# Query, key and value products of two attention heads made among the delta rule's fillers and kept in DRAM

## The chip, the cores and the metric

The kernel runs on one core of a Trainium2 chip. A core has TensorE (matmuls into PSUM), VectorE, ScalarE and GpSimd (element-wise work), and SyncE, which issues nearly all DMAs here from one queue in order. The five run on their own and wait for each other by semaphores. The metric is the device time of one execution in microseconds (us); the kernel before takes 2994.62 us, the median of 3 runs (2992.21 to 2998.93).

## The reference, cut to what matters

One layer of an encoder block in float32, 1024 tokens of width 1024. A normed input is projected once; the columns of the projection feed differential attention (8 heads), a bidirectional gated delta rule (8 heads), and gates. The two branches are projected, gated, summed and projected again; 16 experts with expert choice follow.

```python
h = rmsnorm(x, norm1_w[l])
p = jnp.einsum('bsd,dn->bsn', h, w_in[l])
(qa, ka, va, qkv_g, z, a_f, a_b, b_f, b_b, gate_a, gate_g) = jnp.split(p, split_at, axis=-1)
qa = apply_rope(qa.reshape(b, s, DA_HEADS, 2, DA_DH), cos, sin)
ka = apply_rope(ka.reshape(b, s, DA_HEADS, 2, DA_DH), cos, sin)
...
oa = diff_attention(qa, ka, va, lam)          # softmax(q1 k1) - lam softmax(q2 k2), times v
...
o_fwd = gated_delta_rule_chunked(qg, kg, vg, g_f, beta_f)
o_bwd = flip(gated_delta_rule_chunked(flip(qg), flip(kg), flip(vg), flip(g_b), flip(beta_b)))
...
merged = jax.nn.sigmoid(gate_a) * ya + jax.nn.sigmoid(gate_g) * yg
x = x + jnp.einsum('bsd,de->bse', merged, w_out[l])
x = x + expert_choice_ffn(h2, w_router[l], w_gate[l], w_up[l], w_down[l])
out = rmsnorm(x, norm_f_w)
```

## The kernel before, in words

**How the program is recorded.** Every part of the work is a Python generator (a task). The class `Emit` holds a clock for each engine and a table of costs; of all operations whose inputs are known it records the one that could start first by these clocks, and at a tie the one of the smaller priority number. What comes out is one fixed order of instructions for each engine. On the chip each engine works through its order and waits where an operand is not there. All matmuls of the program come from line 403 (`mm`), all transposes on TensorE from line 407 (`tr`), ScalarE's work from line 415, VectorE's products and sums from line 421, GpSimd's from 425, VectorE's three-operand operations from 446, its reductions from 463, and SyncE's DMAs from 495. So a row of the profile is told by its operands.

**Tags.** A tag is a named place in SBUF with a number of slots; `e.new(tag)` waits until a slot is free and nothing that lies over it is live. `xp` (two slots, the inputs of the delta rule's convolution) and `ax` (two slots of 1024 columns, the attention's projected query, key or value, transposed) lie over each other in block B3. `QS`, `K1`, `K2` (rotated queries and keys) lie in block B1 and can only be taken once all the delta rule's buffers there are done.

**Dense jobs.** A projection job (`proj_ns`) makes a 128 x 1024 slice of the projection: two halves of 512 columns, each 8 x 3 matmuls of 128x512 in float32r (the input and the weights are split in a high and a low part, tiles A0 and A1, and three of the four products are taken), so 48 matmuls a job, named psum<-A,W. `Dense` keeps two queues. `main` holds the delta rule's q, k, v, z jobs and then the attention's jobs, three for each head; `fill` holds the 16 gate jobs, each of which ends in a tanh by ScalarE and a store of 256 KB for each half to `dgate`. The loader looks at the first two of `main`, and takes the first of `fill` when neither may start. The worker has the lowest priority (9), so that dense matmuls go where the planner sees TensorE free.

**The seam.** The attention's jobs may start when the last delta head has its q, k and v (`gdn_close`) and, from head 2 on, when 4 rows of the heads before are done. A job's product goes to an `ax` slot; then `rope` (for q and k) copies it by four DMAs into `rot` with the halves of 32 swapped, multiplies by cosine and sine and adds (three products of 128x1024 on VectorE), and splits the result in high and low parts (ScalarE casts, VectorE and, for a key's second copy, GpSimd subtract); `vrows` transposes the values on TensorE. A head's rows start when it has q, k and v. Three lanes take the 64 rows (8 heads x 8 blocks of 128 queries) in order: scores (8 matmuls psum<-B 128x512), two maxima on VectorE, two exponentials on ScalarE, a scaling, a difference, 8 transposes, 8 matmuls with the values. So a row is 24 instructions of TensorE in the planner's count. Meanwhile `finish` of delta head 7 norms its output (products on VectorE), transposes it by two times four transposes on TensorE, gates it and stores it to `dog`.

Of the kernel before, what the change touches and what calls it, by code (L numbers as in the profile page):

```python
# [8 lines left out]
F32 = mybir.dt.float32  # L9
# [9 lines left out]
S, D, H, P = 1024, 1024, 8, 128  # L19
# [5 lines left out]
AHEAD = 2  # L25
TAIL = 4
LANES = 3
PACE = (4, 4, 4)


# [30 lines left out]
class Buf:  # L61
    def __init__(self, v, slot):
        self.v, self.slot = v, slot
# [654 lines left out]
def proj_ns(g, evac, wait=None):  # L718

    e = g.e  # L720

    def job(hi, lo):
        hh, hl = g.hh, g.hl
        for sh in range(2):
            if not g.hready[sh]:
                yield lambda: g.hready[sh]
            ps = yield from e.new("mm", [P, 512])
            if sh == 0:
                dst = (yield from wait()) if wait else None
            sl = slice(sh * 512, sh * 512 + 512)  # L730
            for d in range(8):
                e.mm3(ps.v, hi[:, d, :], lo[:, d, :], hh[:, d, sl], hl[:, d, sl], d == 0, d == 7)
                yield
            e.urgent(True)
            yield from evac(sh, ps, dst)
            e.free(ps)
            e.urgent(False)
            yield
    return job
# [149 lines left out]
class Head:  # L889
# [8 lines left out]
    def has(self, *f):  # L898
        return all(x in self.flags for x in f)

    def set(self, f):
        self.g.e.then(lambda: self.flags.add(f))
# [347 lines left out]
class Attn:  # L1250
    def __init__(self, g, h, prev):
        self.g, self.h = g, h
        self.pp = prev.prev if prev else None
        self.prev = prev
        self.flags = set()
        self.rows_left = NT

    def has(self, *f):
        return all(x in self.flags for x in f)
# [8 lines left out]
    def jobs(self):  # L1268
        g, h, e = self.g, self.h, self.g.e
        out = []  # L1270
        for j in (0, 1, 2):
            def ok(j=j):
                return g.gdn_close and (not self.pp or 16 - self.pp.rows_left - self.prev.rows_left >= PACE[j])
            def evac(sh, ps, x, j=j):
                e.cp(x[:, sh * 512:sh * 512 + 512], ps.v)
                if sh == 1:
                    e.spawn(self.vrows(x) if j == 2 else self.rope(j, x), 2)
                yield
            out.append((g.ins["w_att"][h, j], ok, proj_ns(g, evac, lambda: e.new("ax", [P, S])), "ax"))
        return out  # L1280

    def vrows(self, x):
        g, e = self.g, self.g.e
        self.v = yield from e.new("v", [P, NT, P])
        self.last("v", "ax")
        for half in range(2):
            pt = yield from e.new("ga", [P, 512])
            for i in range(4):
                t = half * 4 + i
                e.tr(pt[:, i * P:(i + 1) * P], x[:, t * P:(t + 1) * P], g.ident.v)  # L1290
            e.cp(self.v[:, half * 4:half * 4 + 4, :], pt.v.rearrange("p (t x) -> p t x", x=P))
            e.free(pt)
            yield
        e.free(x)
        self.set("v")
# [131 lines left out]
def attn_lane(g, rows, i):  # L1427
    e = g.e
    while rows:
        at, qt = rows.popleft()  # L1430
        yield lambda: at.has("q", "k", "v")
        if qt == 0:
            yield from at.start()
        yield lambda: at.has("start")
        yield from at.row(qt)
    e.then(lambda: setattr(g, "lanes", g.lanes + 1))
    if i == 0:
        yield lambda: g.attn_done == g.heads
        e.close("ga", "sc", "p", "pT", "rsm", "o", "o2", "osm", "aq", "cos", "sin")
        e.free(g.cos, g.sin)  # L1440
# [86 lines left out]
def w_out(g):  # L1527
    e = g.e
    yield lambda: g.lanes == LANES
    for n in range(8):  # L1530
# [566 lines left out]
def body(tc, ins, out, dbg=None, heads=H):  # L2097
    nc = tc.nc
    g = Ctx()
    g.nc, g.tc, g.ins, g.out, g.dbg, g.heads = nc, tc, ins, out, dbg or {}, heads  # L2100
    with ExitStack() as ctx:
# [3 lines left out]
        dp = ctx.enter_context(tc.tile_pool(name="dr", bufs=1, space=DRAM))  # L2105
        e = g.e = Emit(nc, pool, psum)
# [3 lines left out]
        g.dw = [dp.tile([16, 64, 2, 16], F32, name=f"dw{i}") for i in range(2)]  # L2110
        g.dog = dp.tile([2, H, P, S], F32, name="dog")
        g.doa = dp.tile([2, H, P, S], F32, name="doa")
        g.dgate = dp.tile([2, 8, P, S], F32, name="dgate")
        g.dyg = dp.tile([2, 8, P, 512], F32, name="dyg")
        g.dx2 = dp.tile([S, D], F32, name="dx2")
# [28 lines left out]
        d = g.dense = Dense(g)  # L2144
        d.main.append(logit_job(g))
        prev, hs = None, []
        for h in range(heads):
            prev = Head(g, h, prev)
            hs.append(prev)
            j = prev.jobs()  # L2150
# [10 lines left out]
        for h in range(heads):  # L2161
            prev = Attn(g, h, prev)
            ats.append(prev)
            j = prev.jobs()
            d.main.extend(j)

        g.hT_jobs = 0
        d.main = deque(using_hT(g, j) for j in d.main)
# [12 lines left out]
        rows = deque((at, qt) for at in ats for qt in range(NT))  # L2181
        for i in range(LANES):
            e.spawn(attn_lane(g, rows, i), 1)
# [8 lines left out]
        x = Experts(g)  # L2192
# [79 lines left out]
```

## Time and profile before

| what | us |
|---|---|
| median of 3 runs | 2994.62 |
| the runs | 2992.21 to 2998.93 |
| the profiled execution, whole | 3000.25 |
| its span, first to last instruction | 2998.0 |
| delta rule with its projections, to | about 959 |
| attention and the branches' projections, to | about 1800 |
| work before the experts, to | about 1930 |
| experts, to the end | about 2998 |

The span is what the profile's times count from; 2.25 us of the profiled execution lie around it. The limits of the stages are read from the table of stretches and the timelines. Busy shares are of the span. A matmul's record lasts longer than its turn, since matmuls are pipelined: what counts is from one start to the next. The number in brackets behind a timeline row is how long the engine stood still before it, and who ended that.

### The profile page before, as it was taken

The page shows a single profiled execution, that of the slowest core. Times are in us where ns is not written, and L with a number is a line of the kernel's source. Part 1 is how long each engine was busy: PE and PEld are TensorE (multiplying, and loading weights), DVE is VectorE, ACT ScalarE, POOL GpSimd, SP SyncE. Part 2 cuts the span into 40 slices and gives each one's busy share as a digit, 9 for nine tenths or more (in the row PEclk, how much of TensorE's full clock was granted, in tenths as well). Part 3 has the DMA queues.
Part 4 walks back from the last instruction along what each step waited for, and adds up shares of the span by engine and source line. Part 5 has one row for each costly group of instructions (what it writes and reads, how often), then busy time and mean ns, then how long its engine had stood idle before and what let it go on. Part 6 is the DMA issues. An engine that isn't in the chain of part 4 may idle for free.

```text
span 2998.0 us, 40541 instructions
## 1 busy us (share of the span) xinstructions
PE 2855.3 (95%) x14712; PEld 2384.8 (80%) x14712; DVE 2351.6 (78%) x3954; ACT 1760.6 (59%) x2683; POOL 555.9 (19%) x443
## 2 busy tenths in 40 slices
PE   7999999999999899999999998999999999999996
PEld 6787887787788778888888787688888888888885
DVE  7768778677765877877763439899999999999998
ACT  4435445445434566776672322577777777777775
POOL 3322222122222211211125422100000000000001
PEclk9999999999999999999999998999999999999998
DMA  4223322322322111111267833999999999999996
GB/s 141 51 63 92 85 53 65 88 60 62 83 57 79 51 50 51 49 50 43 67 193 238 267 131 137 419 411 386 384 378 388 388 388 388 385 386 381 380 375 244
DMA packets 203642, 598.73 MB, mean 200 GB/s; under 512 B 84386, under 2 KB 102306, under 8 KB 154290
## 3 DMA queue, kind: packets, MB, share of 16 engines
q1 hardware_dynamic: 189858, 562.06, 51.5%
q0 software_dynamic: 13584, 34.08, 4.2%
q8 instruction: 115, 1.88, 0.3%
q14 instruction: 85, 0.70, 0.1%
HBM read 535.19 MB, written 52.49 MB: 196 GB/s over the span
## 4 chain that ended last, share of the span: by engine, by line
PE 70%; DVE 14%; DMA 5%; ACT 3%; issue 2%; SPq 1%; POOL 0%; POOLq 0%; DVEq 0%; ACTq 0%
PE psum L403 65%; DVE B L421 6%; PE psum L407 5%; DVE B L446 5%; DVE B L463 2%; ACT B L415 2%; SPq L495 1%; ACT psum L415 1%; DMA dyg<-W 1%; DMA B<-in_w_out_dram 1%; DMA A<-dh,C 1%; DMA W<-dgate 0%; DVE B L467 0%; DMA dw<-B 0%; DMA doa<-C 0%
## 5 line engine op out<-in xcount | busy, mean ns | idle before, releaser
L403 PE MATMUL psum<-A,W 128*128 128x512 f32 (+1 forms) x5808 | 1518.9, 402 | 11.0 <-POOL W L425 6.0
L403 PEld LDWEIGHTS psum<-A,W 128*128 128x128 f32 (+1 forms) x5808 | 1059.6, 189 | 203.1 <-POOL W L425 9.2
L403 PE MATMUL psum<-B 128*128 128x128 f32 (+3 forms) x3494 | 658.9, 324 | 14.9 <-DVE B L467 7.6
L403 PEld LDWEIGHTS psum<-B 128*128 128x128 f32 x3494 | 544.6, 191 | 89.8 <-DVE B L467 11.1
L415 ACT ACTIVATE B<-B 128x2048 fp32r<-128x2048 f32 (+6 forms) x346 | 381.5, 1106 | 224.1 <-DVE B L446 80.7
L415 ACT ACTIVATE B<-psum 128x512 f32<-128x512 f32 (+4 forms) x614 | 267.2, 441 | 330.4 <-PE psum L403 158.8
L425 POOL TENSOR_TENSOR W<-W,W 128x1024 fp32r<-128x1024 f32 (+1 forms) x105 | 266.1, 2535 | 946.2 <-ACT W L415 820.2
L421 DVE TENSOR_TENSOR B<-B,B 128x2048 fp32r<-128x2048 f32 (+2 forms) x188 | 369.2, 1964 | 43.0 <-ACT B L415 37.2
L403 PE MATMUL psum<-B,W 128*128 128x512 f32 x1488 | 348.5, 390 | 0.0
L403 PEld LDWEIGHTS psum<-B,W 128*128 128x128 f32 x1488 | 279.4, 188 | 58.6 <-DVE B L421 0.4
L415 ACT ACTIVATE B<-psum,B 128x128 f32<-128x128 f32 (+2 forms) x264 | 191.0, 728 | 196.5 <-PE psum L403 122.4
L407 PE MATMUL psum<-C,B 128*128 128x128 f32 (+1 forms) x1392 | 221.0, 283 | 66.2 <-DVE B L446 28.3
L403 PE MATMUL psum<-A,B 128*128 128x512 f32 x1048 | 277.6, 403 | 0.0
L421 DVE TENSOR_TENSOR A<-B,A 128x2048 fp32r<-128x2048 f32 x110 | 251.0, 2289 | 18.9 <-ACT A L415 18.9
L407 PEld LDWEIGHTS psum<-C,B 128*128 128x128 f32 (+1 forms) x1392 | 167.8, 144 | 120.1 <-DVE B L446 36.1
L415 ACT ACTIVATE A<-B 128x2048 fp32r<-128x2048 f32 (+1 forms) x120 | 223.3, 1861 | 64.5 <-PE psum L403 51.7
L403 PE MATMUL psum<-B,B 128*128 128x128 f32 (+1 forms) x1056 | 228.5, 304 | 12.8 <-DVE B L472 10.6
L403 PEld LDWEIGHTS psum<-A,B 128*128 128x128 f32 x1048 | 193.6, 188 | 41.9 <-issue 5.7
L403 PEld LDWEIGHTS psum<-B,B 128*128 128x128 f32 x1056 | 181.7, 192 | 47.9 <-DVE B L472 13.9
L509 POOL DMA_INDIRECT dx<-B,C x15 | 23.8, 1585 | 938.7 <-ACT B L415 938.7
L463 DVE TENSOR_REDUCE B<-psum 128x1 f32<-128x1024 f32 (+1 forms) x136 | 157.2, 1157 | 49.4 <-PE psum L403 48.5
L425 POOL TENSOR_TENSOR B<-B,B 128x128 f32<-128x128 f32 (+2 forms) x96 | 120.9, 1263 | 307.6 <-ACT B L415 217.7
(118 smaller groups left out, 2839.2 us busy)
## 6 DMA issues: line engine op xcount, KB each, us to landing
B<-in_w_gu_dram SPq DMA_DIRECT2D x152, 1024.0 KB, 7.5
A<-in_w_gu_dram SPq DMA_DIRECT2D x79, 1024.0 KB, 7.7
B<-in_w_dn_dram SPq DMA_DIRECT2D x76, 1024.0 KB, 7.1
A<-in_w_dn_dram SPq DMA_DIRECT2D x38, 1024.0 KB, 6.4
W<-in_w_gu_dram SPq DMA_DIRECT2D x25, 1024.0 KB, 7.5
W<-in_w_gdn_dram SPq DMA_DIRECT2D x32, 512.0 KB, 3.7
B<-dG SPq DMA_DIRECT2D x32, 512.0 KB, 5.0
W<-in_w_proj_dram SPq DMA_DIRECT2D x32, 512.0 KB, 4.4
```

The source lines that it names most:

```text
L403: self.op("pe", c, lambda: self.nc.tensor.matmul(out, lhsT, rhs, start=start, stop=stop), [out], [lhsT, rhs], l, "mm")
L407: self.op("pe", 109, lambda: self.nc.tensor.transpose(out, in_, ident), [out], [in_, ident], 55, "tr")
L415: self.op("act", c, lambda: self.nc.scalar.activation(out, in_, func, **kw), [out] + w, [in_] + r, 0, "act")
L421: self.op("dve", 69 + 1.041 * free(out), lambda: self.nc.vector.tensor_tensor(out, a, b, op), [out], [a, b], 0, "tt")
L425: self.op("pool", 150 + 2.104 * free(out), lambda: self.nc.gpsimd.tensor_tensor(out, a, b, op), [out], [a, b], 0, "ptt")
L446: lambda: self.nc.vector.scalar_tensor_tensor(out, a, s, b, op0=op0, op1=op1),
L463: self.op("dve", 69 + 1.041 * free(in_), lambda: self.nc.vector.tensor_reduce(out, in_, axis=AX.X, op=op), [out], [in_], 0, "red")
L495: self.op("sp", 478, lambda: self.nc.sync.dma_start(out, in_), [out], [in_], 0, "dma", max(n / (375.0 if self.real else 360.0), 112))
L509: self.op("pool", 1100, lambda: self.nc.gpsimd.indirect_dma_start(out=dst, out_offset=bass.IndirectOffsetOnAxis(ap=idx, axis=0), in_=y, in ...
```

## The change

For the first two attention heads (SPILLED = 2) the three projection jobs leave `main` and are put into `fill` behind the tenth gate job. Such a job needs no `ax` slot and doesn't wait for `gdn_close`: each half is copied by ScalarE from PSUM to a `gst` buffer (as a gate job does with its tanh) and stored to a new DRAM tensor `dqkv`. When both halves are stored, a task `fetch` is started: it waits for `gdn_close` (head 1 also for all three of head 0), takes an `ax` slot, loads the 128 x 1024 product back by one DMA, and goes on with `rope` or `vrows` as before. In all, 12 stores of 256 KB and 6 loads of 512 KB are added; nothing is removed.

```diff
--- before.py
+++ after.py
@@ -25,6 +25,7 @@
 AHEAD = 2
 TAIL = 4
 LANES = 3
+SPILLED = 2
 PACE = (4, 4, 4)
 
 
@@ -1254,6 +1255,7 @@
         self.prev = prev
         self.flags = set()
         self.rows_left = NT
+        self.left = 3
 
     def has(self, *f):
         return all(x in self.flags for x in f)
@@ -1276,8 +1278,30 @@
                 if sh == 1:
                     e.spawn(self.vrows(x) if j == 2 else self.rope(j, x), 2)
                 yield
-            out.append((g.ins["w_att"][h, j], ok, proj_ns(g, evac, lambda: e.new("ax", [P, S])), "ax"))
+            def spill(sh, ps, _, j=j):
+                th = yield from e.new("gst", [P, 512])
+                e.cp(th.v, ps.v)
+                e.dma(g.dqkv[h, j, :, sh * 512:sh * 512 + 512], th.v)
+                e.free(th)
+                if sh == 1:
+                    e.spawn(self.fetch(j), 2)
+            if h < SPILLED:
+                out.append((g.ins["w_att"][h, j], lambda: True, proj_ns(g, spill), None))
+            else:
+                out.append((g.ins["w_att"][h, j], ok, proj_ns(g, evac, lambda: e.new("ax", [P, S])), "ax"))
         return out
+
+    def fetch(self, j):
+
+        g, e = self.g, self.g.e
+        if not g.gdn_close or self.prev and not self.prev.has("fetched"):
+            yield lambda: g.gdn_close and (not self.prev or self.prev.has("fetched"))
+        x = yield from e.new("ax", [P, S])
+        e.dma(x.v, g.dqkv[self.h, j])
+        self.left -= 1
+        if self.left == 0:
+            self.set("fetched")
+        yield from (self.vrows(x) if j == 2 else self.rope(j, x))
 
     def vrows(self, x):
         g, e = self.g, self.g.e
@@ -2110,6 +2134,7 @@
         g.dw = [dp.tile([16, 64, 2, 16], F32, name=f"dw{i}") for i in range(2)]
         g.dog = dp.tile([2, H, P, S], F32, name="dog")
         g.doa = dp.tile([2, H, P, S], F32, name="doa")
+        g.dqkv = dp.tile([SPILLED, 3, P, S], F32, name="dqkv")
         g.dgate = dp.tile([2, 8, P, S], F32, name="dgate")
         g.dyg = dp.tile([2, 8, P, 512], F32, name="dyg")
         g.dx2 = dp.tile([S, D], F32, name="dx2")
@@ -2162,7 +2187,11 @@
             prev = Attn(g, h, prev)
             ats.append(prev)
             j = prev.jobs()
-            d.main.extend(j)
+            if h < SPILLED:
+                for i in range(3):
+                    d.fill.insert(10 + 3 * h + i, j[i])
+            else:
+                d.main.extend(j)
 
         g.hT_jobs = 0
         d.main = deque(using_hT(g, j) for j in d.main)
```

What the recorded order makes of it is shown at three places. The first is TensorE in the seam: rows of psum<-A,W are dense matmuls, the x4 rows psum<-C,B are head 7's transposes (C holds the unit matrix). Before, from the end of the job ahead of the first transposes to a little behind them:

```order
...
L403 MATMUL psum<-A_78,W_111 128x512 x2
L403 MATMUL psum<-A_79,W_111 128x512
L403 MATMUL psum<-A_78,W_111 128x512
L407 MATMUL psum<-C_76,B_80 128x128 x4
L403 MATMUL psum<-A_78,W_111 128x512
L403 MATMUL psum<-A_79,W_111 128x512
...
L403 MATMUL psum<-A_79,W_111 128x512
L403 MATMUL psum<-A_78,W_111 128x512 x2
L407 MATMUL psum<-C_76,B_80 128x128 x4
L403 MATMUL psum<-A_79,W_111 128x512
L403 MATMUL psum<-A_78,W_111 128x512 x2
...
```

With the change the same place:

```order
...
L404 MATMUL psum<-A_79,W_112 128x512 x2
L404 MATMUL psum<-A_80,W_112 128x512
L404 MATMUL psum<-A_79,W_112 128x512
L408 MATMUL psum<-C_77,B_81 128x128 x4
L404 MATMUL psum<-A_79,W_112 128x512
L404 MATMUL psum<-A_80,W_112 128x512
...
L404 MATMUL psum<-A_80,W_112 128x512
L404 MATMUL psum<-A_79,W_112 128x512
L408 MATMUL psum<-C_77,B_81 128x128 x4
L404 MATMUL psum<-A_79,W_112 128x512
L404 MATMUL psum<-A_80,W_112 128x512
...
```

Since the last matmul of the delta rule's chains 77 dense matmuls stand ahead of the first transposes before, and 98 now; between the two groups of transposes 16 and 15; from there to the values' transposes 32 and 49; behind these none and two until the first attention row.

The second place is TensorE some 100 attention instructions into the first rows (psum<-B 128x512 scores, psum<-B 128x128 products with the values, psum<-C,B transposes of a row). Before:

```order
L403 MATMUL psum<-B_80 128x128 x4
L403 MATMUL psum<-A_79,W_111 128x512
L403 MATMUL psum<-A_78,W_111 128x512 x2
L403 MATMUL psum<-A_79,W_111 128x512
L403 MATMUL psum<-B_80 128x128 x4
L403 MATMUL psum<-B_7778 128x512 x8
L403 MATMUL psum<-B_80 128x128 x8
L403 MATMUL psum<-A_78,W_111 128x512
L407 MATMUL psum<-C_76,B_80 128x128 x4
L403 MATMUL psum<-A_78,W_111 128x512
L403 MATMUL psum<-A_79,W_111 128x512
```

With the change:

```order
L404 MATMUL psum<-A_79,W_112 128x512
L404 MATMUL psum<-B_81 128x128 x8
L404 MATMUL psum<-B_7785 128x512 x4
L408 MATMUL psum<-C_77,B_81 128x128 x8
L404 MATMUL psum<-B_7785 128x512 x4
L408 MATMUL psum<-C_77,B_81 128x128 x8
L404 MATMUL psum<-B_81 128x128 x8
L404 MATMUL psum<-B_7785 128x512 x5
L408 MATMUL psum<-C_77,B_81 128x128 x4
L404 MATMUL psum<-B_7785 128x512 x3
L404 MATMUL psum<-B_81 128x128 x4
L408 MATMUL psum<-C_77,B_81 128x128 x4
```

The run of attention instructions goes on for four more rows of the order, 80 instructions in all with no dense matmul between; before, the longest such run in the first rows is 20. Until the 112th attention instruction 91 dense matmuls stand between before, and 57 and the eight transposes of head 1's values now.

The third place is SyncE's queue around the small stores and loads of delta head 7 (dl), with the change:

```order
L496 DMA W_84<-in_w_att_dram 128x1024 x2
L496 DMA dqkv<-W_84 128x512
L496 DMA B_83<-dqkv 128x1024 x2
L496 DMA dl_67<-B_82 16x16x16 x2
L496 DMA dqkv<-W_84 128x512
L496 DMA dl_67<-B_82 16x16x16 x2
L496 DMA W_84<-in_w_gates_dram 128x1024
L496 DMA dl_67<-B_82 16x16x16 x4
L496 DMA B_81<-dl_67 64x16x16 x2
```

Before, gate weights and dgate stand where attention weights and dqkv stand now, and the row B<-dqkv x2 is not there. Later, in the seam:

```order
L496 DMA B_81<-B_83 32x1024 x8
L496 DMA dgate<-W_84 128x512
L496 DMA W_84<-in_w_gates_dram 128x1024
L496 DMA B_83<-dqkv 128x1024
L496 DMA dgate<-W_84 128x512 x2
L496 DMA dog<-B_81 128x256 x2
L496 DMA B_83<-dqkv 128x1024
L496 DMA dog<-B_81 128x256 x2
L496 DMA dgate<-W_84 128x512
L496 DMA B_81<-B_83 32x1024 x4
L496 DMA dog<-B_81 128x256 x2
L496 DMA dgate<-W_84 128x512
```

The loads from dqkv are head 0's values and head 1's queries, the x8 and x4 rows B<-B the swapped copies for rope, dog the output of delta head 7.

## Rows read from the trace of the kernel before

**Rows 1.** The page, part 1, and of part 2 the granted clock of TensorE.

```profile
PE 2855.3 (95%) x14712; PEld 2384.8 (80%) x14712; DVE 2351.6 (78%) x3954; ACT 1760.6 (59%) x2683; POOL 555.9 (19%) x443
PEclk9999999999999999999999998999999999999998
```

**Rows 2.** The page, part 4: the chain that ended last, by engine.

```profile
PE 70%; DVE 14%; DMA 5%; ACT 3%; issue 2%; SPq 1%; POOL 0%; POOLq 0%; DVEq 0%; ACTq 0%
```

**Rows 3.** Stretches: busy us and instructions by engine, TensorE clock, DMA, GB/s.

```profile
885.00:958.95 73.95, 72.25 (x452) 64.11 (x453) 35.39 (x118) 30.44 (x82) 14.25 (x6) 0.98 0.28 80
958.95:1001.38 42.43, 32.93 (x144) 26.69 (x143) 29.26 (x40) 15.51 (x35) 12.51 (x4) 0.88 0.26 71
1001.38:1044.14 42.76, 42.76 (x238) 36.44 (x237) 36.55 (x50) 29.62 (x51) 8.65 (x3) 1.00 0.21 56
1083.51:1123.62 40.11, 34.10 (x184) 28.50 (x182) 33.74 (x49) 26.05 (x47) 5.42 (x2) 0.91 0.22 67
1930.00:2930.00 1000.00, 1000.00 (x4573) 824.82 (x4572) 915.08 (x556) 759.38 (x513) 59.74 (x28) 1.00 0.99 384
```

**Rows 4.** Timeline of TensorE, 959 to 1001: start, length, what, pause before.

```profile
958.95 17.74 PE L403 MATMUL psum<-A,W 128*128 128x512 f32 x77
985.39 1.11 PE L407 MATMUL psum<-C,B 128*128 128x128 f32 x4 [8.70 <-DVE B L421]
986.16 5.83 PE L403 MATMUL psum<-A,W 128*128 128x512 f32 x16
992.79 0.66 PE L407 MATMUL psum<-C,B 128*128 128x128 f32 x4 [0.80 <-DVE B L446]
993.21 7.55 PE L403 MATMUL psum<-A,W 128*128 128x512 f32 x32
1000.59 1.04 PE L407 MATMUL psum<-C,B 128*128 128x128 f32 x8
```

**Rows 5.** Timeline of VectorE in the same stretch.

```profile
967.35 1.22 DVE L421 TENSOR_TENSOR B<-B,B 128x1024 f32<-128x1024 f32 x1 [0.18 <-DMA B<-B]
...
984.11 7.84 DVE L421 TENSOR_TENSOR B<-B,B 128x1024 f32<-128x1024 f32 x3
991.98 0.75 DVE L446 SCALAR_TENSOR_TENSOR B<-psum,C,B 128x512 f32<-128x512 f32 x1
...
1002.59 1.22 DVE L463 TENSOR_REDUCE B<-psum 128x1 f32<-128x1024 f32 x1 [0.30 <-PE psum L403]
```

**Rows 6.** Timeline of GpSimd in the same stretch.

```profile
984.56 6.31 POOL L425 TENSOR_TENSOR B<-B,B 64x1024 fp32r<-64x1024 f32 x2 [2.33 <-ACT B L415]
```

**Rows 7.** Timeline of the DMA queue of SyncE, 962 to 1001.

```profile
962.96 10.47 SPq L495 DMA_DIRECT2D B<-B  x8
973.48 0.57 SPq L495 DMA_DIRECT2D W<-in_w_att_dram  x1
993.21 7.02 SPq L495 DMA_DIRECT2D dog<-B  x6
```

**Rows 8.** The page, part 6, and its longer answer: DMA issues, KB, us to landing.

```profile
W<-in_w_att_dram SPq DMA_DIRECT2D x24, 512.0 KB, 3.9
dgate<-W SPq DMA_DIRECT2D x32, 256.0 KB, 2.1
dog<-B SPq DMA_DIRECT2D x64, 128.0 KB, 2.2
B<-in_c_cos_dram SPq DMA_DIRECT2D x1, 512.0 KB, 4.6
```

**Rows 9.** Timeline of VectorE at 845.

```profile
844.84 1.22 DVE L446 SCALAR_TENSOR_TENSOR B<-B,B 128x1024 f32<-128x1024 f32 x1
```

**Rows 10.** Timeline of the DMA queue of SyncE at 852.

```profile
851.90 0.95 SPq L495 DMA_DIRECT2D dl<-B  x2
```

**Rows 11.** Timeline of TensorE at 1114.

```profile
1113.94 1.12 PE L407 MATMUL psum<-C,B 128*128 128x128 f32 x4 [3.61 <-DVE B L440]
1114.71 3.34 PE L403 MATMUL psum<-A,W 128*128 128x512 f32 x7
```

## The prediction

> **What bounds the kernel now.** I read the page first, then the chain of waits, then the table of stretches around the place that the change touches, then the timelines of TensorE, VectorE, GpSimd and the DMA queue there. The page shows TensorE busy 95% of the span at nearly full clock [rows 1], and the chain that ended last is TensorE for 70% of it and VectorE for 14% [rows 2]. So the kernel is a queue of matmuls, and a change that keeps every matmul, as this one does, can only win or lose the time in which TensorE stands still. The stretches say where that is. In the 74 us before 958.95, with the delta rule of the last two heads and fillers between, TensorE is busy 72.25; the experts' 1000 us have no pause at all [rows 3]. Between 958.95 and 1001.38 it is busy 32.93 of 42.43 us, and its clock is at 0.88 on average [rows 3]. That is the seam: the last chain of the delta rule is done, and the first attention row has not begun.
>
> In the seam TensorE runs 77 matmuls of projections, pauses 8.70 us for VectorE, does four transposes of head 7's finish and 16 matmuls, pauses 0.80 us, does the other four transposes and 32 matmuls, and then the value transposes of head 0 [rows 4]. VectorE is the chain here: from 967.35 it works through rope of head 0 and the finish of head 7. The product that the first transposes wait for is the first of the three that start at 984.11; the second transposes wait for the one that ends at 992.73 [rows 5]. The three products take 7.84 us, 2.6 each, where the same size takes 1.22 alone [rows 5]; GpSimd subtracts in the same 6.31 us [rows 6]. The change touches none of that.
>
> **The change, part by part.**
>
> *Fillers before 959 us.* The order of the instructions is the same on TensorE, VectorE, ScalarE and GpSimd up to the last gated projection of head 7: six attention projections stand where six gate jobs stood, with the same 48 matmuls each, one evacuation of 512 columns by ScalarE and one store of 256 KB per half. I cost this at nothing. Only SyncE's queue differs: the loads of head 0's query and key products, 512 KB each, stand ahead of the small stores of the last delta head. They wait for the last reader of the convolution's buffer, which ends at 846.06 [rows 9]; those stores do not start before 851.90 [rows 10], and such a load lands in 3.9 to 4.6 us [rows 8]. The cover is 5.8 us. If it fails, the price is at most one such load behind the other, 4.6 us on the last delta head.
>
> *The seam.* The six gate jobs left over now stand where the projections of heads 0 and 1 stood. A gate job needs no buffer of the attention, so it can stand earlier: 98 matmuls ahead of the first transposes instead of 77. At 17.74 / 77 = 0.230 us each [rows 4] they last 22.6 us, to 981.5, and the pause falls from 8.70 to some 3.9 us. Before the second transposes stand 15 matmuls instead of 16, and these transposes come at 992.79 in both, because VectorE sets that. So there TensorE is 21 - 1 = 20 matmuls ahead: 4.6 us gained. The granted clock of this place doesn't enter: if the 15 matmuls again take the 5.83 / 16 = 0.364 us each that they have now [rows 4], they are done in 5.5 us, before VectorE is. The seam's whole idle time, 42.43 - 32.93 = 9.5 us [rows 3], is the most that fillers can give here, and half of it stays because the order still puts the transposes before the rest of the fillers.
>
> The Trainium skill (Trainium Kernel Development and Optimization, "Performance Expectations") wants the room of TensorE read from the weight loads' busy time and not from the matmuls'. The seam has 26.69 us of it in 42.43, the experts 824.82 in 1000 [rows 3]; by that rule the seam's room would be 42.43 - 26.69 / 0.825 = 10.1 us, against 9.5 by the idle time, and the sum the same, since VectorE's product holds the place in both readings.
>
> Then come 49 matmuls instead of 32, at 7.55 / 32 = 0.236 us [rows 4], the value transposes (0.79 us, 1000.59 to 1001.38), and two more matmuls. The first attention row starts at 993.21 + 11.6 + 0.8 + 0.5 = 1006.1, 4.7 us later than now, with 20 + 17 + 2 = 39 matmuls more behind it.
>
> *Loads.* Head 0's values and head 1's products are fetched when rope has let go of its two buffers. SyncE's queue is in order, so behind head 1's query load wait two stores of head 7's output and a gate's store; the rotation behind it waits for the load. Now these stores go from 993.21 over 7.02 us [rows 7]. The load goes out at about 994.2, lands after 4.6 us [rows 8], and the rotation (eight of which take 10.47 us now with their waits [rows 7]) ends, landing included, near 1003.5 (another 128 KB lands in 2.2 us [rows 8]), before the first row's scores (1006.1 + 1.2). I cost it at nothing; each us beyond that delays VectorE, since two products of head 1's rope now stand ahead of the first row's maximum.
>
> *The first rows.* Here the gain is partly given back. From the first attention matmul to the 112th attention instruction TensorE now has 91 matmuls of projections between; after the change it has 57 and eight value transposes, and 80 attention instructions follow each other with no filler. What stood there has been spent earlier, in the seam. At that point the new order is 39 - 34 = 5 matmuls and eight transposes further, 5 x 0.23 + 0.8 = 1.9 us of TensorE. When does it get there? Now: 1044.14. The trace shows no such stretch without fillers, so I bound it. TensorE alone needs 137 x 0.23 + 40 x 0.1 = 35.5 us (a transpose is 0.79 / 8 = 0.1), so 1041.6 at the earliest. VectorE is busy 36.55 of the 42.76 us now [rows 3]; three operations of rope at 1.22 us [rows 5] move ahead of the first row, so 32.9 remain from 1006.1 + 1.2 = 1007.3, to 1040.2; with the 6.2 us of pauses that it has now, to 1046.4. Gain at that point: 1.9 + 1044.14 - 1041.6 = 4.4 at best, 1.9 + 1044.14 - 1046.4 = -0.4 at worst. I take 2.0, the middle, because both ends rest on the same row, once without its pauses and once with all of them.
>
> *Afterwards.* The order of TensorE differs up to the work before the experts and is the same from there on; the order of the rest of attention is redrawn with the same instructions. I cost that at zero, with about 6 us either way: the pauses from 1083.51 to 1123.62 alone are 6.0 us with a clock of 0.91 [rows 3].
>
> **Sum.** The profiled execution took 3000.25 us (span 2998.0 and 2.25 around it), 5.6 more than the median of 2994.62. 3000.25 - 2.0 = 2998.2 for a like execution; against the median 2994.62 - 2.0 = 2992.6, which I predict.
>
> **Rivals.**
> *B, more is won.* The redrawn rows lie further ahead of the projections (the last attention instruction comes 28 instructions earlier in TensorE's order), so later stalls find more fillers. If the best end (4.4) holds and the 6.0 us of pauses of 1083.51 to 1123.62 go too, it is 10.4 us: 2984.2. For it: that pause (3.61 us, VectorE [rows 11]) is of the kind that fillers cover. Against: its neighbours change at random.
> *C, it is all given back.* VectorE keeps its pauses in the first rows, the worst end: 2995.0. For it: rope of head 1 and the rows want VectorE at once, and TensorE now arrives later with less to do meanwhile.
> *D, slower.* The 80 attention instructions without a filler: there a wait of a row for VectorE or ScalarE is a pause of TensorE, and the clock falls with it, as at 1113.94: 3.61 us, and then 7 matmuls in 3.34, 0.48 each [rows 11]. The stretch around that one lost 6.0 + 0.09 x 40.11 = 9.6 us [rows 3]. One such stretch in the first rows and a second pause like that (3.6 + 7 x 0.25 = 5.4) less the 4.6 of the seam: 10.4 slower, 3005.0. The Trainium skill would expect this side: Perfetto Trace Analysis, "Optimization Strategy", says that where the most contended engine changes over time, interleaving such regimes may help, and the change takes 34 matmuls out from beside the rows. It decides from the point where new pauses in the 45 us after the first row exceed 4.6 us.
> *E, the change does not do what it says:* the early loads hold SyncE's queue, the cover of 5.8 us fails, and the last delta head is late by up to 4.6 us: with nothing won, 2999.2.
>
> **How the numbers follow.** Forecast A 0.43, B 0.25, C 0.17, D 0.11, E 0.04. About 0.2%, 6 us, is what a measurement of this kernel can tell from no change (its three runs lie 6.7 us apart). A, C and E lie within it, but for 0.03 on either side, where the redrawn order carries them over; B is faster, D slower. So faster 0.25 + 0.03 = 0.28, slower 0.11 + 0.03 = 0.14, same 0.58. The range reaches to B and most of the way to D: 2983 to 3002.
>
> **What would show it.** Right: nothing moves before 959; the pause before head 7's first transposes is 3 to 5 us; the second transposes still follow VectorE's product; the first row's scores at about 1006; projections of head 2 near 1044; the experts as long as now and starting some 2 us earlier. Wrong: a pause above 6 us in the seam, VectorE waiting for the load of head 1's products, or TensorE pauses above 4.6 us between 1006 and 1050.

## The result and the profile after

The changed kernel takes 3017.88 us (median of 4 runs, 3016.32 to 3019.28), the kernel before 2995.03 in runs beside it: ratio 1.0072, 95% interval 1.006 to 1.0084. It is 22.9 us slower, where I had forecast 2.0 us faster and a range that ended at 3002. The profiled execution took 3019.28 us, its span 3017.5.

The page of the changed kernel, the engines' busy time and the chain by engine, to hold against [rows 1, 2]; the same 14712 matmuls are busy for 10.1 us longer:

```profile
PE 2865.4 (95%) x14712; PEld 2389.6 (79%) x14712; DVE 2357.0 (78%) x3954; ACT 1761.5 (58%) x2683; POOL 556.4 (18%) x443
...
PE 71%; DVE 13%; DMA 5%; ACT 3%; issue 2%; SPq 1%; POOL 0%; POOLq 0%; DVEq 0%; ACTq 0%
```

The stretches of the changed kernel, columns as in [rows 3] (the fourth has no counterpart there):

```profile
885.00:958.95 73.95, 71.77 (x450) 63.25 (x448) 36.02 (x121) 30.14 (x81) 14.25 (x6) 0.98 0.31 94
958.95:1005.76 46.81, 41.89 (x181) 34.09 (x181) 32.83 (x43) 17.95 (x38) 14.56 (x5) 0.93 0.44 129
1005.76:1050.00 44.24, 38.75 (x214) 32.27 (x213) 33.60 (x48) 30.53 (x51) 5.67 (x2) 0.96 0.28 81
...
1490.00:1545.00 55.00, 47.15 (x260) 38.54 (x259) 40.04 (x66) 35.04 (x67) 16.04 (x12) 0.91 0.69 194
...
1950.00:2950.00 1000.00, 1000.00 (x4576) 824.54 (x4575) 915.36 (x557) 760.09 (x514) 57.45 (x27) 1.00 0.99 384
```

The delta rule and the experts are as they were. The seam has become denser (41.89 of 46.81 us busy instead of 32.93 of 42.43). The first rows had no idle time before and have 44.24 - 38.75 = 5.5 us now, and around 1500 a stretch of 55 us stands still for 7.9 with the clock at 0.91.

To see where the loss arises I count TensorE's work in both traces, every matmul at the usual spacing of its shape, and ask when each kernel has done the same amount. The changed kernel is then later by:

| time in the kernel before | 959 | 1008 | 1044 | 1114 | 1284 | 1294 | 1497 | 1541 | 1854 | 1938 |
|---|---|---|---|---|---|---|---|---|---|---|
| later by, us | 0.9 | -3.7 | 4.7 | -1.2 | 2.7 | 6.7 | 7.5 | 17.5 | 18.8 | 21.1 |

From the end of the delta rule to the last of these places both kernels run the same 4904 matmuls, first the kernel before, then the changed one (columns as in [rows 3]):

```profile
958.95:1938.00 979.05, 929.30 (x4904) 769.79 (x4903) 680.08 (x1231) 533.38 (x950) 249.02 (x207) 0.98 0.40 131
```

```profile
959.84:1959.10 999.26, 936.79 (x4904) 773.19 (x4903) 684.30 (x1231) 533.13 (x950) 249.41 (x207) 0.97 0.41 134
```

Of the 20.2 us that the changed kernel takes longer here, 12.7 are standing still and 7.5 are longer busy time of the same matmuls, at a granted clock of 0.97 instead of 0.98. So a pause costs more than its own length.

The seam gives 0.9 + 3.7 = 4.6 us, as forecast. The first rows take 8.4. After them comes one gain, where the stall of the kernel before at 1113.94 [rows 11] has no counterpart, and then losses in steps: 4 us up to 1284, 4 near 1290 and 10 near 1500.

What TensorE waits for between the first row and the router's work, first in the kernel before, then in the changed one (L446 there is L447 here, scalar_tensor_tensor; L415 and L416 ScalarE):

```profile
engine line waited for: us in total, times, longest us
PE psum L407 <- DVE B L446: 6.5, 8, 2.1
PE psum L407 <- DVE B L440: 5.6, 4, 3.6
...
PE psum L403 <- ACT B L415: 4.8, 5, 1.6
```

```profile
PE psum L408 <- DVE B L447: 13.8, 7, 3.7
PE psum L404 <- ACT B L416: 11.1, 9, 2.3
...
PE psum L408 <- DVE B L441: 2.7, 2, 2.5
PE psum L408 <- DMA B<-dqkv: 1.6, 1, 1.6
```

The round trip through DRAM shows with one wait of 1.6 us. What has grown is two waits: for VectorE's three-operand products, the difference of the two exponentials of an attention row (13.8 us instead of 6.5), and for ScalarE (11.1 instead of 4.8).

### The profile page after: what moved, and what is told of

It reads as the page before. It is cut to its first block, busy times and chain, and to the rows that moved or that the text cites. A ratio compares the mean times of both kernels' runs of the same rounds, so it can differ in the third digit from the quotient of the medians.

```text
span 3017.5 us, 40574 instructions
## 1 busy us (share of the span) xinstructions
PE 2865.4 (95%) x14712; PEld 2389.6 (79%) x14712; DVE 2357.0 (78%) x3954; ACT 1761.5 (58%) x2683; POOL 556.4 (18%) x443
## 3 DMA queue, kind: packets, MB, share of 16 engines
q8 instruction: 115, 1.88, 0.3%
## 4 chain that ended last, share of the span: by engine, by line
PE 71%; DVE 13%; DMA 5%; ACT 3%; issue 2%; SPq 1%; POOL 0%; POOLq 0%; DVEq 0%; ACTq 0%
PE psum L404 66%; DVE B L422 5%; PE psum L408 5%; DVE B L447 4%; ACT B L416 2%; DVE B L464 2%; DMA dyg<-W 1%; SPq L496 1%; ACT psum L416 1%; DMA dw<-B 0%; DMA A<-dh,C 0%; DVE B L468 0%; DMA B<-B 0%; POOL W L426 0%; DMA B<-dG 0%
## 5 line engine op out<-in xcount | busy, mean ns | idle before, releaser
L404 PEld LDWEIGHTS psum<-A,W 128*128 128x128 f32 (+1 forms) x5808 | 1061.0, 189 | 208.8 <-POOL W L426 10.1
L404 PE MATMUL psum<-B 128*128 128x128 f32 (+3 forms) x3494 | 662.1, 326 | 22.6 <-ACT B L416 11.1
L416 ACT ACTIVATE B<-B 128x2048 fp32r<-128x2048 f32 (+6 forms) x346 | 381.6, 1106 | 218.5 <-DVE B L447 78.2
L416 ACT ACTIVATE B<-psum 128x512 f32<-128x512 f32 (+4 forms) x602 | 261.0, 439 | 318.1 <-PE psum L404 149.1
L416 ACT ACTIVATE B<-psum,B 128x128 f32<-128x128 f32 (+2 forms) x264 | 191.1, 728 | 206.7 <-PE psum L404 123.7
L416 ACT ACTIVATE A<-B 128x2048 fp32r<-128x2048 f32 (+1 forms) x120 | 223.4, 1862 | 65.1 <-PE psum L404 52.2
L404 PEld LDWEIGHTS psum<-B,B 128*128 128x128 f32 x1056 | 180.5, 191 | 46.7 <-DVE B L473 12.7
```

The lines of the kernel that those rows point to most:

```text
L404: self.op("pe", c, lambda: self.nc.tensor.matmul(out, lhsT, rhs, start=start, stop=stop), [out], [lhsT, rhs], l, "mm")
L416: self.op("act", c, lambda: self.nc.scalar.activation(out, in_, func, **kw), [out] + w, [in_] + r, 0, "act")
```

## The experiments

Two theories stood against each other. T1, my rival D: the change takes fillers from beside the rows, and that costs. T2: the planner that writes the order draws the whole order of attention anew once something moves at the seam, and the kernel before is a fortunate draw. The planner keeps a clock for each engine; put ahead once by some us at the start of a head's attention, it writes another order with the same instructions. So one kernel can be given the other's order. The kernel before, measured beside them, took 2993.75 (with late_order, last_order, spread and draw2), 2995.74 (with hold, draw2_spill, draw3_spill and vrope) and 2995.97 (with late_vrope and the three other kernels whose names end in vrope).

**The changed kernel's order without the change (late_order).**

```
 before, Attn.start():
+        if self.h == 0:
+            e.clk["dve"] += 4000
```

> The kernel before, without spilled projections; only the planner's clock of VectorE is put 4 us ahead once, when the attention of head 0 begins. No instruction is added or taken away. Its order is that of the kernel before up to the first attention row, and word for word that of the changed kernel on TensorE, VectorE, ScalarE and GpSimd from about 1045 us on to the end. Theory T1 (my rival D: fillers taken from beside the rows leave pauses and a slow clock): here the fillers of the seam and the first rows are those of before, so 2995, within 6. Theory T2 (the price lies in the redrawn order after the first rows, which any small push at the seam draws anew): between 1049 us and the experts the changed kernel fell 16 us behind the one before, and the same order must lose them here: 3011, within 5. What is left up to 3018 is then the change's own part.

Measured: 3017.07, ratio 1.0074 (1.0057 to 1.009). All of the loss is there, with no projection spilled. T1 falls, as far as it means the change itself; at the same late order the two kernels differ by 0.8 us. T2's own number, 3011 within 5, was too low: this kernel loses 7.7 us in the first rows as well (1.1 late at 1008, 8.8 at 1044), where T1's condition doesn't quite hold either, since its trace has a run of 64 attention instructions with no projection between (from 1039.5; the kernel before has 20, the changed one 80). The same kernel measured once more (in late_vrope, against its name, nothing is moved to VectorE):

> late_order once more, one look, for the scatter of its pauses: the same places as before (3.2 at 1209, 2.4 at 1296, 2.9 at 1442, 3.8 at 1514), 3017 within 4.

3019.85, with the same waits.

**Only the last part of that order (last_order).**

```
 before, Attn.start():
+        if self.h == 1:
+            e.clk["act"] += 3000
```

> The kernel before; the planner's clock of ScalarE is put 3 us ahead once, when head 1's attention begins. Order of before up to about 1060 us, word for word the changed kernel's on all engines from about 1292 us on. T1: 2995, within 6. T2: the changed kernel stood 6.7 us behind at 1292 us and 21.1 at the experts, so that last part brings 14: 3009, within 5.

Measured: 3009.13, 1.0051 (1.0034 to 1.0068), as T2 had it. By the count of work its trace is 2.0 us late at 1294, 0.1 at 1497, 9.5 at 1541 and 10.9 at 1938: the step near 1500 came along, the smaller ones of the changed kernel behind 1294 not all. One pause tells how faithfully the order carries a stall along. It stands before the transposes of a row of the seventh head, in late_order, last_order, spread (below) and the changed kernel:

```profile
1513.53 0.55 PE L407 MATMUL psum<-C,B 128*128 128x128 f32 x3 [3.83 <-DVE B L446]
```

```profile
1502.92 0.55 PE L407 MATMUL psum<-C,B 128*128 128x128 f32 x3 [3.80 <-DVE B L446]
```

```profile
1511.15 0.55 PE L408 MATMUL psum<-C,B 128*128 128x128 f32 x3 [3.73 <-DVE B L447]
```

```profile
1510.26 0.90 PE L408 MATMUL psum<-C,B 128*128 128x128 f32 x3 [3.74 <-DVE B L447]
...
1533.40 3.40 PE L404 MATMUL psum<-B 128*128 128x512 f32 x8 [1.88 <-ACT B L416]
```

The pause (3.73 to 3.83) belongs to the order, not to the change and not to the execution.

**Another order of the first rows (spread).**

```
 changed, Attn.start():
+        if self.h == 0:
+            e.clk["act"] += 4000
```

> The changed kernel; the planner's clock of ScalarE is put 4 us ahead once at the start of head 0's attention. No instruction is added or taken away; TensorE's order differs only over 250 instructions in the first rows: the run of 80 attention instructions without a filler becomes one of 36 at most, with the same fillers; from about 1073 us on every engine's order is the changed kernel's. T1: the run of 80 is what costs; of the 12 us lost between 990 and 1049 us two thirds come back: 3010. T2: the first rows matter little beside the later order: 3018, within 4.

Measured: 3018.21, 1.0085 (1.0067 to 1.0103). But the kernel is not what I had expected of it. In its trace no matmul of a projection stands between the row of six and the row of two below. Between them lie 27 us (1028.76 to 1055.67) and some 85 instructions, where the changed kernel has its 80 in 22 us (1029.68 to 1051.63). So the run did not shrink to 36, and a longer pause stands in it:

```profile
1025.73 1.64 PE L404 MATMUL psum<-A,W 128*128 128x512 f32 x6
...
1035.18 1.11 PE L408 MATMUL psum<-C,B 128*128 128x128 f32 x4 [5.22 <-DVE B L447]
...
1055.67 0.72 PE L404 MATMUL psum<-A,W 128*128 128x512 f32 x2
```

So this run decides nothing on rival D, nor on the rule that I had named with it (the Trainium skill, Perfetto Trace Analysis, "Optimization Strategy"), that interleaving may help: fillers spread more evenly in the first rows, with all else the same, were not run.

**Gate jobs held back for the first rows (hold).**

```
 changed, body():
-                d.fill.append(gate_job(g, k, n))
+                w, _, f, b = gate_job(g, k, n)
+                d.fill.append((w, (lambda: ats and ats[0].has("start"))
+                               if 2 * n + k >= 13 else (lambda: True), f, b))
```

> The changed kernel, but the last three gate jobs may load only when head 0's attention has begun: they stand beside the first rows instead of in the seam (65, 53, 69, 65 dense matmuls per 96 attention instructions instead of 65, 28, 90, 50, and no run without a filler longer than 32), and the whole order behind is drawn anew. T1: what the change took from the first rows is back, the seam's gain of 4.6 is lost: 2997. T2: it is one more draw: 2995 to 3020, I take 3008.

Measured: 3023.29, 1.0082 (1.0063 to 1.0101), outside of what either theory allowed, since the seam itself broke: the held jobs left TensorE with nothing to do there.

```profile
985.96 2.82 PE L408 MATMUL psum<-C,B 128*128 128x128 f32 x12 [6.23 <-DVE B L447]
...
1003.48 2.08 PE L404 MATMUL psum<-B 128*128 128x512 f32 x4 [11.50 <-ACT B L416]
```

By the count of work it is 20.2 us late at 1008, still 20.2 at 1065 and 23.9 at 1938. Its first rows, with no run longer than 32, lost nothing, and its later order, one more draw, cost 3.7. But it came to these rows 20 us later, so the fillers are not the only difference.

**More draws, with the change and without.** draw2 is the kernel before with `e.clk["act"] += 2000` at head 0, draw2_spill the changed one with `e.clk["dve"] += 4000` at head 1, draw3_spill the changed one with `e.clk["act"] += 1500` at head 0.

> The kernel before; the planner's clock of ScalarE is put 2 us ahead once at the start of head 0's attention: a third draw of the order after the first row, with as many fillers beside the rows as before (92, 41, 75, 64 per 96 attention instructions). T1: 2995, within 6, as nothing is taken from beside the rows. T2: the draws scatter; 2995 to 3015, I take 3005.

Measured: 3009.82, 1.0053 (1.0034 to 1.0072), against T1 and within what T2 allowed.

> The changed kernel with the planner's clock of VectorE put 4 us ahead once at the start of head 1's attention: seam and first rows of the changed kernel, and from about 1290 us on word for word the order of draw2 on TensorE, VectorE, ScalarE and GpSimd. T2 (the late order sets the time; the change's own part is about nothing, 3017.9 against 3017.1): as draw2, 3010, within 5. T1 (spilled projections cost 20 us whatever the order): 3018 to 3030.

Measured: 3001.55, 1.0016 (1.0006 to 1.0025). Better than I had said by more than the 5 us allowed: the two share their order only from 1290 on, and 8 us of difference are there by 1313, most of it one pause before the same transposes (6.58 us at 1293.71 in draw2, 1.44 at 1288.17 here). So the same order does not always cost the same: it also counts how late each engine comes to it.

> The changed kernel with the planner's clock of ScalarE put 1.5 us ahead once at the start of head 0's attention: from the first row on a draw of the order that no other kernel here has; no instruction more or less. T2: anywhere between 2993 and 3018, and I take 3003; the change is then not what made 3018. T1: 3013 or more, as the fillers taken from beside the first rows are gone here too.

Measured: 3007.13, 1.0031 (1.002 to 1.0042), again against T1 and within T2's wide range. The four orders without the change lie at 2995 (before), 3009, 3010 and 3017, those with it at 3002, 3007, 3018 and 3018 (spread shares the changed kernel's from 1073 us on; hold, with its broken seam, is left aside). The two groups overlap; before is the fastest of its own group. These are not eight independent draws: late_order, last_order and spread carry the late order of the changed kernel, draw2_spill that of draw2.

**What makes an order dear (vrope).** Ahead of the pause at 1510.26 VectorE and GpSimd both subtract for the key rope of the last head. VectorE of the changed kernel:

```profile
1502.24 6.64 DVE L422 TENSOR_TENSOR B<-B,B 64x1024 fp32r<-64x1024 f32 x2
...
1508.92 1.28 DVE L447 SCALAR_TENSOR_TENSOR B<-B,B 128x1024 f32<-128x1024 f32 x1
```

and GpSimd:

```profile
1502.13 5.67 POOL L426 TENSOR_TENSOR B<-B,B 64x1024 fp32r<-64x1024 f32 x2 [10.40 <-ACT B L416]
```

Two subtractions take 3.3 us each, and the row's product at 1508.92, for which TensorE has stood since 1506.5, is queued behind them. At 1204.77 and 1292.05, with pauses of 3.20 and 2.36 us, it is the row's own product that is stretched beside GpSimd's subtractions, and ahead of the second a product of one column takes 2.04 us (0.16 at 1502.05):

```profile
1201.46 3.25 DVE L447 SCALAR_TENSOR_TENSOR B<-B,B 128x1024 f32<-128x1024 f32 x1
...
1285.39 2.04 DVE L422 TENSOR_TENSOR B<-B,C 128x1 f32<-128x1 f32 x1
...
1288.71 3.28 DVE L447 SCALAR_TENSOR_TENSOR B<-B,B 128x1024 f32<-128x1024 f32 x1
```

The pause of the kernel before at 1113.94 [rows 11] has the same cause:

```profile
1110.63 3.25 DVE L446 SCALAR_TENSOR_TENSOR B<-B,B 128x1024 f32<-128x1024 f32 x1
```

In the next kernel GpSimd's two products, still planned as GpSimd's, are issued on VectorE, so that the order of the program stays as the planner wrote it:

```
 changed:
+    def vptt(self, out, a, b, op):
+        self.op("pool", 150 + 2.104 * free(out), lambda: self.nc.vector.tensor_tensor(out, a, b, op),
+                [out], [a, b], 0, "ptt")
 Attn.rope():
-            e.ptt(k2[lo, 0], x[lo], f32(k1[lo, 0]), ALU.subtract)
-            e.ptt(k2[hi, 1], x[hi], f32(k1[hi, 1]), ALU.subtract)
+            e.vptt(k2[lo, 0], x[lo], f32(k1[lo, 0]), ALU.subtract)
+            e.vptt(k2[hi, 1], x[hi], f32(k1[hi, 1]), ALU.subtract)
```

> The changed kernel in its own order on TensorE, ScalarE and SyncE; the two products that GpSimd subtracts in each head's key rope are issued on VectorE instead (16 instructions of 64x1024, at 1.22 us alone). Theory P: the long pauses of TensorE (3.20 at 1204, 2.36 at 1292, 2.93 at 1438, 3.74 at 1510) are rows queued on VectorE behind rope's products, which take 2.0 to 3.4 us beside GpSimd's instead of 1.22. Each head then holds VectorE for 4.9 us instead of 6.6 at the worst; these four pauses shrink by half, with their slow clock: 3010. Rival: VectorE is simply full there, 19.5 us more of work on it make the pauses longer: 3022 or more.

Measured: 3000.08, 1.0006 (0.9996 to 1.0017): of the loss of 22.9 us all but 4.3 is gone, more than I had expected. For the work of the 999.26 us above it takes 983.75 (957.05 to 1940.80), with 933.13 busy: 11.9 us less standing still and 3.7 less busy time. Of the five pauses above 2.2 us that the changed kernel has behind 1100 one is left (2.45 at 1427). The same place in this kernel, VectorE (L430 are the two products that came from GpSimd, L451 is the row's product):

```profile
1491.05 1.22 DVE L422 TENSOR_TENSOR B<-B,B 64x1024 fp32r<-64x1024 f32 x1
1492.28 1.22 DVE L430 TENSOR_TENSOR B<-B,B 64x1024 fp32r<-64x1024 f32 x1
1493.53 1.22 DVE L422 TENSOR_TENSOR B<-B,B 64x1024 fp32r<-64x1024 f32 x1
...
1494.79 1.29 DVE L451 SCALAR_TENSOR_TENSOR B<-B,B 128x1024 f32<-128x1024 f32 x1
1496.10 1.22 DVE L430 TENSOR_TENSOR B<-B,B 64x1024 fp32r<-64x1024 f32 x1
```

and TensorE, the transposes that wait for it:

```profile
1496.13 0.55 PE L408 MATMUL psum<-C,B 128*128 128x128 f32 x3 [0.80 <-DVE B L451]
```

Ahead of the row's product now stand three subtractions of 3.7 us together instead of two of 6.64, and the pause is 0.80 instead of 3.74. Of the 10 us that the changed kernel lost near 1500 this takes 4.3 back. ScalarE's wait behind it, 1.88 us at 1533.40 above, stands in vrope as well (1.88 at 1517.60).

Is this a gain of its own, or one that belongs to the changed kernel's order? The same edit in the other kernels:

> The kernel before in its own order; only the two products per head that GpSimd subtracts in the key rope are issued on VectorE. Theory P (pauses of TensorE come from rows queued on VectorE behind rope's products, which are slow beside GpSimd's): before had fewer such pauses, 1.60 at 1046, 3.61 at 1114 and 2.06 at 1424, and the seam; some 5 us of them with their clock go: 2990. Rival: the gain of 18 in the changed kernel was one more lucky shift and nothing general: 2995 or more.

Measured: 2992.63, 0.9987 (0.9975 to 0.9999): 3.3 us, between the two expectations, and the only kernel here that is faster than before. Its pause of 3.61 us at 1113.94 has shrunk to 0.93 (at 1106.27).

> late_order (no spilled projections, the changed kernel's order from about 1045 us on) with rope's GpSimd products on VectorE. P: as the changed kernel with the same edit, 3000, plus the change's own part that shows at equal order without these pauses; the seam gave the spilled one 4 us up to 1450: 3003, within 4. Rival: the 18 us do not come back here: 3012 or more.

Measured: 3001.58, 1.0021 (1.001 to 1.0032): 15.5 us back, within what was expected. Without these pauses, too, the change is worth little at the same late order: 3000.08 against 3001.58.

> draw2_spill (the change, in the better draw, 3001.6) with rope's GpSimd products on VectorE. P: its pauses 1.94 at 990, 2.51 at 1034, 2.36 at 1209, 1.44 at 1288, 2.62 at 1524 shrink by half, with the clock: 2993, the fastest so far with the change. Rival: this order has little left to win: 3000.

Measured: 2998.34, 1.0008 (0.9996 to 1.0021): between the two expectations, nearer to the rival's. The edit gives 18 and 15.5 us in the dear order, 3 in each of the two cheap ones. The four kernels with it lie within 9 us of each other; the same four without it within 23.

How slow the subtractions are does not tell these orders apart. All of size 64x1024 from 1001 to 1560 us, in the kernel before, the changed one, and with GpSimd's products on VectorE (total and mean ns):

```profile
L421 DVE TENSOR_TENSOR B<-B,B 64x1024 fp32r<-64x1024 f32 x28 | 48.4, 1729 | 3.3 <-ACT B L415 2.5
```

```profile
L422 DVE TENSOR_TENSOR B<-B,B 64x1024 fp32r<-64x1024 f32 x28 | 46.4, 1657 | 2.0 <-ACT B L416 1.2
```

```profile
L422 DVE TENSOR_TENSOR B<-B,B 64x1024 fp32r<-64x1024 f32 x28 | 34.1, 1220 | 1.9 <-ACT B L416 1.2
L430 DVE TENSOR_TENSOR B<-B,B 64x1024 fp32r<-64x1024 f32 x14 | 17.0, 1218 | 0.3
```

Before pays as much for GpSimd's company (1.73 us each) as the changed kernel (1.66). Where the stretched ones fall is what counts: at the four pauses above, on a row's product or just ahead of it, at a moment when TensorE's order has no other work to go on with.

What is left after that edit, 3000.08 against 2992.63, stands with ScalarE in the waits of TensorE, first in vrope and then in before_vrope:

```profile
PE psum L404 <- ACT B L416: 9.5, 11, 1.9
PE psum L408 <- DVE B L451: 7.7, 7, 2.4
```

```profile
PE psum L407 <- DVE B L450: 8.5, 9, 2.5
...
PE psum L403 <- ACT B L415: 3.2, 5, 1.1
```

For VectorE they now wait alike; for ScalarE 6.3 us more. No run took these waits away, so why they fall so in that order stays open.

## Why the prediction was wrong

*Fillers before 959.* Right: 0.9 us at 959, in the scatter of an execution (the traces of the other kernels lie there from 3.7 us ahead to 1.2 behind).

*The seam.* Right, in the mechanism and in the sizes. TensorE in the changed kernel, to hold against [rows 4]:

```profile
959.84 22.50 PE L404 MATMUL psum<-A,W 128*128 128x512 f32 x98
986.28 1.11 PE L408 MATMUL psum<-C,B 128*128 128x128 f32 x4 [3.94 <-DVE B L422]
987.04 5.65 PE L404 MATMUL psum<-A,W 128*128 128x512 f32 x15
993.68 0.66 PE L408 MATMUL psum<-C,B 128*128 128x128 f32 x4 [0.98 <-DVE B L447]
994.09 11.40 PE L404 MATMUL psum<-A,W 128*128 128x512 f32 x49
1005.33 1.03 PE L408 MATMUL psum<-C,B 128*128 128x128 f32 x8
```

98 matmuls in 22.5 us, a pause of 3.94 (3.9 forecast), the second transposes where VectorE sets them, the first row's scores at 1006.67 (1006.1 forecast), and 4.6 us gained. One reading was wrong without harm here: the three products of [rows 5] are not 2.6 us each. The first, which the transposes wait for, takes 1.23, and two subtractions of 64x1024 behind it take 3.28 each.

*Loads.* Nearly right. Head 1's queries and keys cost nothing. Its values were overlooked: they are fetched only when a buffer of rope is free again, and 1.65 us of pause wait for them. SyncE's queue:

```profile
994.99 0.40 SPq L496 DMA_DIRECT2D B<-dqkv  x1
...
1006.67 0.35 SPq L496 DMA_DIRECT2D B<-dqkv  x1
...
1013.98 0.39 SPq L496 DMA_DIRECT2D B<-dqkv  x1
```

and TensorE:

```profile
1018.78 0.66 PE L408 MATMUL psum<-C,B 128*128 128x128 f32 x4 [1.65 <-DMA B<-dqkv]
```

*The first rows.* Mis-sized. I had the gain at 1044 between -0.4 and 4.4 and took 2.0; it was a loss of 4.7 - 0.9 = 3.8. My worst end gave the new order the pauses of the old one and no more. It had 5.5 us of them and the clock at 0.96. The stretch where projections become scarce is real. Between 1008 and 1065 every order with 36 or more attention instructions in a row there (draw2 36, draw3_spill 56, late_order 64, changed 80, spread more) loses 6.5 to 11.4 us, and those with 20 or 32 (last_order, hold) lose nothing; vrope, with its 80, loses 8.0, so rope's subtractions on GpSimd are not the reason at this place. That such a run is the cause is not shown, since these orders differ in more than the run; and it is not the change's own, since late_order has it with nothing spilled.

*Afterwards: the step that failed.* I wrote that the redrawn order costs zero, 6 us either way. From 1044 to the experts it cost 21.1 - 4.7 = 16.4, and late_order shows the whole loss with the order alone. The 6 us came from one stretch with a pause, the one at 1113.94 [rows 3, 11]. But I had its cause in hand: [rows 5, 6] show VectorE's products slowed beside GpSimd's subtractions (to 2.6 us as I read it, to 3.28 in truth, instead of 1.22), and each of eight heads brings two such subtractions. A redraw moves all of them against the rows; the changed kernel has pauses of 2.3 to 3.7 us at five places behind 1100 (1125, where ScalarE ends the wait, 1205, 1292, 1439 and 1510), the kernel before at one (3.61 at 1114). I had also written that such a change can only win or lose the time in which TensorE stands still; 7.5 of the 20.2 us lost behind the delta rule are longer busy time of the same matmuls. One stretch lost 9.6 by my own count; a few of them, more or fewer, make 10 to 20 us either way, not 6.

*The rivals.* B and C lie on the wrong side. D had the right sign and too small a part. Its point of decision, 4.6 us of new pauses in the 45 us after the first row, was passed (5.5), and the stretch that it priced at 9.6 us took 8.4. But the changed kernel is ahead again by 1114, where the kernel before has its own such stretch, and late_order loses 7.7 at the same place without the change. D ended at 3005; the greater part of the loss came behind 1114. E did not occur. No case stood for a dear draw of the whole order. It should have, and on both sides: the draws that were run lie from 2995 to 3018.

*The change's own part.* At the same late order it is 3017.88 against 3017.07, and 3000.08 against 3001.58 with the other products moved: nothing that these runs can tell from zero or from my sum of -2.0. Of the seam's gain the changed kernel is still 4.2 us ahead of late_order at 1250, 2.0 at 1670, and nothing at 1695. The last step is one of the clock: both wait 1.7 us for GpSimd there (at 1673.63 and 1675.14), but only the changed kernel's clock falls in the 10 us behind (0.83 from 1672 to 1682; late_order 1.00 from 1673 to 1683). Each is one execution.

## What to carry to other kernels

Where a planner orders the instructions, a change at one place is priced together with the order that it draws for everything behind it: run the kernel before in a few nudged orders first, and take their scatter (here 23 us) as the width of the forecast. To tell a change from its draw, give the old kernel the new order by a nudge that adds no work. And look for what makes the draws differ: here two engines that slow each other, at a place where a row waits; moving that work to one engine narrowed the scatter of four kernels from 23 us to 9. A pause of TensorE is to be priced with the slower clock beside it, which was more than a third of the loss here.

## What the hardware showed unexpectedly

VectorE's subtraction of 64x1024 takes 1.22 us alone and up to 3.4 beside GpSimd's, and even a product of 128x1 took 2.04 there; GpSimd's two took 5.67 us in the same place, so the two engines together did four in 6.8 us, which VectorE alone does in 4 x 1.22 = 4.9. Moving GpSimd's share to VectorE, the busier of the two, took the stretching of these subtractions away (all at 1.22 in vrope) and made the kernel up to 18 us faster. The Trainium skill says of this pair (SBUF — State Buffer, "SBUF: two separate sides") that they share ports which one instruction holds whole while the other waits, when VectorE reads two inputs from SBUF and GpSimd reads there too. The rows agree as far as they go: it is VectorE that is stretched, by 2.1 us each, beside GpSimd instructions of 2.8, and a product of 128x1 that takes 2.04 us instead of 0.16 looks like such a wait. It also says (Perfetto Trace Analysis, "Optimizing Scalar/DVE Operations") that shifting work between these two might not help; here shifting it back is what helped.
